# Attention's operands prepared once behind their projection, and a projection moved beside the first attention

## The chip, the cores and the metric

One core of a Trainium2 chip runs the whole kernel. The metric is the device time of one execution in microseconds (us). The kernel before takes 3615.32 us (median of three runs, 3614.81 to 3616.18).

## What is computed

One decoder layer on a prompt of 2048 tokens and on 8 further single tokens (the sample) with a paged cache. Shortened from the reference:

```python
h = rms_norm(x, norm1_g)
aq, ak, av, iq, ik, iw, rq, rf, ri, rg = split(h @ w_in)      # 1024 -> all widths
aq, ak = rms_norm(aq by heads of 64), rms_norm(ak)            # 8 query, 2 key heads
att = attend(aq, ak, av, iq, ik, iw)    # 256 best causal keys by the indexer's score,
                                        # softmax(q.k / 8) over them, times values
rec, S = hgrn2_mixer(rq, rf, ri, rg)    # gated linear recurrence, 4 heads of 128
x = x + concatenate([att, rec]) @ w_out
x = x + square(relu(rms_norm(x) @ w_up)) @ w_down
```

The kernel computes in float32. Where TensorE multiplies, each operand is split in two parts (high: rounded to the engine's fp32r type; low: the rest), and products of parts are summed: three matmuls per product in the projections (function mm3), two in attention, where a stationary operand of 128 rows holds high and low parts of 64 values under each other.

## The kernel before, in words

The prompt is 16 tiles (blocks) of 128 tokens; tile 16 is the sample. The stages, in order of time:

1. Attention's projection (project_tile in attn_proj): for each of three column sets ("k": keys, values, indexer keys; "i": indexer queries; "q": queries) a tile's product goes to PSUM, is normalized, and is stored to DRAM: kD, vD, aqD and others.
2. The recurrence (recur) with the indexer's scores beside it, and the early part of the choice of keys.
3. recurrence_out: for the first EARLY = 10 tiles the recurrent half of the output projection, added to x and stored in yD (line 898). Per tile 4 transposes (line 886) and 24 matmuls of 512 columns (lines 127 to 129). Its weights are loaded as four raw pieces (line 876), rounded by ACT and subtracted by POOL (line 878).
4. Three rounds of attention and MLP, over tiles 0 to 5, 6 to 11 and 12 to 16. For tiles at or past EARLY the MLP stage itself does the recurrent half (ks = 8 in place of 4, line 1660). Steps of the sample's attention (picks; its scores are line 1198) run beside them as tracks, stepped by credit.

Attention keeps keys and values of all blocks so far in SBUF (KS, VS). Each round makes them anew: prep_keys loads a key block, ACT writes its high part (line 103, tile kts), POOL the low part (line 104), TensorE makes four transposes (line 89, tile dt), ACT copies the result out (line 920); values are split by ACT and POOL too (lines 921, 922). prep does it for a block's queries (lines 95, 96, tiles aqs and dt; 8 transposes). So 6, 12 and 16 key blocks are made in the three rounds, 34 in all.

The order on each engine is set at build time by a scheduler with priorities: what stands under high_priority goes ahead, and store() issues its DMA on SP at a low priority. attend(...) in round 0 runs under NEAR, far ahead of the rest. DMAs issued by SP and by POOL stand in those engines' instruction streams, so one that waits holds back what stands behind it.

Of the kernel before, what the change touches and what calls it, by code (L numbers as in the profile page):

```python
# [45 lines left out]
def hymba_kernel(ctx, tc, x_prompt, x_sample, cache_k, cache_v, cache_kidx, state_hgrn, page_table,  # L46
# [99 lines left out]
    def trunk(ctx):  # L146
# [20 lines left out]
        with tc.tile_pool(name="pb", bufs=1, reuse_waits="tile") as pb, ExitStack() as qb_:  # L167
            pj_ = ExitStack()
            pj = pj_.enter_context(tc.tile_pool(name="pj", bufs=1, reuse_waits="tile"))
            with tc.high_priority(offset=HIGH):  # L170
                recur = recurrence(pb, pj)
                finish()
            po_.close()
            qb = qb_.enter_context(tc.tile_pool(name="qb", bufs=1, space=PSUM, reuse_waits="tile"))
            qj = pj_.enter_context(tc.tile_pool(name="qj", bufs=1, space=PSUM, reuse_waits="tile"))
            with tc.high_priority(offset=MIDDLE):
                recur(qb, qj, pj_.close)
                if EARLY:
                    with tc.tile_pool(name="pf", bufs=1, reuse_waits="tile") as pf, \
                         tc.tile_pool(name="qf", bufs=1, space=PSUM, reuse_waits="tile") as qf:  # L180
# [6 lines left out]
        pi_.close()  # L187
        pw = ctx.enter_context(tc.tile_pool(name="pw", bufs=1, reuse_waits="tile"))
        loads = mlp_loads(pw, E_IO, E_WB)
# [29 lines left out]

        with tc.high_priority(offset=FIRST):  # L220
            early = Track(choose_all(choose_block, range(AHEAD)), 0)
            early.finish()
# [65 lines left out]
    PREP = 0  # L288
    EARLY = 10
    yD = dram.tile([NB, P, D], F32, name="yD")  # L290
# [8 lines left out]
    def attn_proj(pc, p1, pr):  # L299
# [82 lines left out]
        def project_tile(t, po, q1, IK, hh, hl, i):  # L382
            n = rows(t)
            rs = slice(row0(t), row0(t) + n)
            for kind, (wh, wl, cols) in (("kiq"[i], weights[i]),):
# [3 lines left out]
                def post():  # L389
                    o = po.tile([P, 512], F32, tag="zo", name="zo", bufs=2)  # L390
                    if kind == "k":
                        head_norm(po, ps[:n, 0:128], n, 2, kg, o[:n, 0:128])
                        head_norm(po, ps[:n, 256:320], n, 1, ig, o[:n, 256:320])
                        nc.scalar.copy(o[:n, 128:256], ps[:n, 128:256])
                        nc.vector.tensor_scalar(o[:n, 320:328], ps[:n, 320:328], IW_SCALE, None, op0=OP.mult)
                        store(kD[rs], o[:n, 0:128])
                        store(vD[rs], o[:n, 128:256])
                        store(iwD[rs], o[:n, 320:328])
                        if t < NB:
                            store(nk_prompt[0, 0, rs].rearrange("s k d -> s (k d)"), o[:n, 0:128])  # L400
                            store(nv_prompt[0, 0, rs].rearrange("s k d -> s (k d)"), o[:n, 128:256])
                            store(ni_prompt[0, 0, rs], o[:n, 256:320])
                            sp = split_twice(po, o[:, 256:320], 1, "iks", 2, nc.gpsimd)
                            pk = q1.tile([P, 512], F32, tag="ikt", name="ikt", bufs=1)
                            for i in range(2):
                                transpose_part(pk[:, i * P:(i + 1) * P], sp[:, 0, i].rearrange("p a d -> p (a d)"))
                            nc.scalar.copy(IK[:, :, rs], pk[:, :2 * P].bitcast(F32R).rearrange("p (i t) -> p i t", i=2))
                        else:
# [461 lines left out]
    def recurrence_out(pf, qf):  # L870
# [3 lines left out]
        for k in range(4):  # L874
            raw = pf.tile([P, D], F32, tag="raw", name="raw", bufs=2)
            nc.sync.dma_start(raw, w_out[0, 512 + k * P:512 + (k + 1) * P])
            nc.scalar.copy(wh[:, k], raw)
            nc.gpsimd.tensor_tensor(wl[:, k], raw, wh[:, k].bitcast(F32), op=OP.subtract)
        for t in range(EARLY):
# [12 lines left out]
            for hf in range(2):  # L892
                s = slice(hf * 512, (hf + 1) * 512)
                po = qf.tile([P, 512], F32, tag="po", name="po", bufs=2)
                for k in range(4):
# [5 lines left out]
    def attend_all(pk, blocks):  # L901

        LEN = (blocks[-1] + 1) * P
        KS = pk.tile([P, NKV, 2, LEN], F32R, name="KS")
        VS = pk.tile([P, blocks[-1] + 1, NKV, P], F32R, name="VS")
        keys = [0]
        VF = pk.tile([P, WHOLE, NKV, HD], F32, name="VF")

        def prep_keys(p2, q2, b, PT):
            rs = slice(b * P, (b + 1) * P)  # L910
            kt = p2.tile([P, NKV * HD], F32, tag="kt", name="kt", bufs=2)
            nc.sync.dma_start(kt, kD[rs])
            vt = VF[:, b] if b < WHOLE else p2.tile([P, NKV, HD], F32, tag="vt", name="vt", bufs=2)
            nc.sync.dma_start(vt.rearrange("p k d -> p (k d)"), vD[rs])
            sp = split_twice(p2, kt, NKV, "kts", 1, nc.gpsimd)
            ps = q2.tile([P, 512], F32, tag="pt", name="dt", bufs=PT)
            for kv in range(NKV):
                for i in range(2):
                    transpose_part(ps[:, (2 * kv + i) * P:(2 * kv + i + 1) * P], sp[:, kv, i].rearrange("p a d -> p (a d)"))
            nc.scalar.copy(KS[:, :, :, rs], ps.bitcast(F32R).rearrange("p (k i t) -> p k i t", k=NKV, i=2))  # L920
            nc.scalar.copy(VS[:, b, :, 0:HD], vt)
            nc.gpsimd.tensor_tensor(VS[:, b, :, HD:], vt, VS[:, b, :, 0:HD].bitcast(F32), op=OP.subtract)

        def prep(p2, q2, cols, b, PT):

            rs = slice(b * P, (b + 1) * P)
            while keys[0] <= b:
                prep_keys(p2, q2, keys[0], PT)
                keys[0] += 1
            aq = p2.tile([P, NH * HD], F32, tag="aq", name="aq", bufs=2)  # L930
            nc.sync.dma_start(aq, aqD[rs])
            n = (b + 1) * P
# [7 lines left out]
            sp = split_heads(p2, aq, NH, "aqs", 1, nc.gpsimd)  # L940
            aqT = p2.tile([P, NH, P], F32R, tag="aqT", name="aqT", bufs=2)
            for q in range(0, NH, 4):
                ps = q2.tile([P, 512], F32, tag="pt", name="dt", bufs=PT)
                for j in range(4):
                    transpose_part(ps[:, j * P:(j + 1) * P], sp[:, q + j].rearrange("p a d -> p (a d)"))
                (nc.vector.tensor_copy if q else nc.scalar.copy)(aqT[:, q:q + 4, :],
                                                                 ps.bitcast(F32R).rearrange("p (h t) -> p h t", t=P))
            return aqT, MB

        def logits(p2, q2, cols, b, u, aqT, MB, LB, out):  # L950
# [4 lines left out]
            for j in range(2):  # L955
                L = p2.tile([P, cols], F32, tag="L", name="L", bufs=LB)
                mx = None
                for k0 in range(0, n, 512):
                    kn = min(512, n - k0)
                    ps = q2.tile([P, 512], F32, tag="lg", name="lg", bufs=2)  # L960
                    for i in range(2):
                        nc.tensor.matmul(ps[:, :kn], aqT[:, 2 * u + j], KS[:, u // 2, i, k0:k0 + kn], start=i == 0, stop=i == 1)  # L962
                    m2 = p2.tile([P, 1], F32, tag="mx", name="mx", bufs=8)
# [10 lines left out]
        def values(p2, q2, b, u, att, PTB, OB, sm, *Ls):  # L974
# [3 lines left out]
            for k0 in range(0, b + 1, 2):  # L978
# [15 lines left out]
                for i in range(m):  # L994
# [4 lines left out]
                    else:  # L999
                        nc.tensor.matmul(O, VS[:, kb, kv], ph[:, s], start=kb == 0, stop=False)  # L1000
                        nc.tensor.matmul(O, VS[:, kb, kv], pl[:, s], start=False, stop=kb == b)
                yield
# [758 lines left out]
```

## Time and profile before

| profiled execution | 3615.09 us (span 3613.4) |
|---|---|
| mean granted TensorE clock | 0.963 of full speed |
| busy, share of the span | PE 93%, PEld 81%, DVE 65%, ACT 62%, POOL 33% |
| projection | 0 to 320 us |
| recurrence, indexer scores | 320 to 1072 |
| recurrence_out, 10 tiles | 1055 to 1126 |
| attention and MLP, round 0 | 1126 to 1286, to 1986 |
| attention and MLP, round 1 | 1986 to 2232, to 2903 |
| attention and MLP, round 2 | 2903 to 3140, to 3613 |

PE is the matmul stream of TensorE, PEld its weight loads, which overlap. A high busy share alone does not say that PE sets the time of a stage: matmuls in a row are pipelined, and a lone one counts with its whole latency. Where PE waits, the row that ends the wait names who was late.

### The profile page before, as it was taken

Reading aid. Unit: us, or ns where it says so; the run is one execution under the profiler, and the core shown is the slowest. Engines: PE = TensorE matmul, PEld = TensorE weight load, DVE = VectorE, ACT = ScalarE, POOL = GpSimd, SP = SyncE. Lnnn points to the kernel's source line nnn. Section 1 sums busy time; section 2 is a strip of 40 time slices with the busy share of each in tenths; the row PEclk is TensorE's granted clock in tenths of the full one; section 3 lists DMA queues with packets and bytes.
Section 4 is the critical chain, followed back from the end, with each engine's and each line's share of the span. In section 5 each row is a group of like instructions: output and inputs, shape, how many; then the busy total and the mean of one; then the engine's idle time right before and its main releaser. Section 6 shows DMA issues by size and latency. Waiting matters only on the chain. (4 is left out here: it accounts for less than half of the span.)

```text
span 3613.4 us, 57448 instructions
## 1 busy us (share of the span) xinstructions
PE 3346.2 (93%) x20446; PEld 2930.4 (81%) x20446; DVE 2333.3 (65%) x5138; ACT 2236.6 (62%) x4121; POOL 1206.7 (33%) x1469
## 2 busy tenths in 40 slices
PE   8998989999998979999999798899799969899999
PEld 7876888899986568888888576888689958788888
DVE  3667788877763656897964578888537448633223
ACT  5788976776753757859832677476695347533332
POOL 5555666554452234444522211113401120011110
PEclk9999999999997989999999899999899979999999
DMA  6546465545445135545544202433434420144554
GB/s 203 147 145 155 140 178 154 154 126 159 129 131 164 57 135 179 167 150 175 163 139 152 65 24 85 135 111 110 154 108 145 135 94 25 62 152 164 186 165 145
DMA packets 345230, 484.90 MB, mean 134 GB/s; under 512 B 39432, under 2 KB 255216, under 8 KB 344816
## 3 DMA queue, kind: packets, MB, share of 16 engines
q1 hardware_dynamic: 287616, 329.37, 28.8%
q0 software_dynamic: 57328, 151.87, 14.2%
q8 instruction: 160, 2.62, 0.3%
q14 instruction: 126, 1.03, 0.1%
HBM read 366.86 MB, written 114.29 MB: 133 GB/s over the span
## 5 line engine op out<-in xcount | busy, mean ns | idle before, releaser
L480 ACT ACTIVATE jkA<-S,candA 128x1152 int8<-128x1152 f32 (+11 forms) x448 | 584.8, 1306 | 116.2 <-DVE candA L484 96.0
L1717 DVE TENSOR_TENSOR y<-y,dn 128x512 f32<-128x512 f32 x512 | 346.1, 683 | 331.1 <-PE dn L129 327.8
L127 PE MATMUL up<-hh,wh 128*128 128x384 f32 (+2 forms) x1536 | 493.4, 321 | 15.0 <-ACT rl L1690 6.9
L128 PE MATMUL up<-hl,wh 128*128 128x384 f32 (+2 forms) x1536 | 491.3, 320 | 0.0
L129 PE MATMUL up<-hh,wl 128*128 128x384 f32 (+2 forms) x1536 | 486.2, 320 | 2.5 <-DMA wl<-low 1.7
L128 PE MATMUL dn<-dl,uh 128*128 128x512 f32 x1024 | 406.5, 397 | 7.2 <-DMA dl<-low 7.2
L127 PE MATMUL dn<-dh,uh 128*128 128x512 f32 x1024 | 403.1, 398 | 10.1 <-DVE y L1717 9.6
L129 PE MATMUL dn<-dh,ul 128*128 128x512 f32 x1024 | 401.2, 394 | 0.0
L127 PEld LDWEIGHTS up<-hh,wh 128*128 128x128 f32 x1536 | 291.9, 190 | 26.7 <-ACT rl L1690 7.4
L128 PEld LDWEIGHTS up<-hl,wh 128*128 128x128 f32 x1536 | 292.2, 190 | 9.0 <-issue 0.3
L129 PEld LDWEIGHTS up<-hh,wl 128*128 128x128 f32 x1536 | 290.1, 190 | 10.5 <-DMA wl<-low 2.0
L1538 ACT CAST dh<-raw 128x1024 fp32r<-128x1024 f32 x96 | 96.9, 1046 | 242.9 <-PE dn L129 231.1
L1693 DVE TENSOR_TENSOR ul<-rl,uh 128x384 fp32r<-128x384 f32 (+1 forms) x192 | 120.7, 629 | 191.7 <-ACT uh L1692 190.5
L127 PEld LDWEIGHTS dn<-dh,uh 128*128 128x128 f32 x1024 | 193.4, 189 | 48.8 <-DVE y L1717 12.3
L129 PEld LDWEIGHTS dn<-dh,ul 128*128 128x128 f32 x1024 | 193.7, 189 | 43.7
L128 PEld LDWEIGHTS dn<-dl,uh 128*128 128x128 f32 x1024 | 194.1, 190 | 40.6 <-DMA dl<-low 7.7
L458 DVE SCALAR_TENSOR_TENSOR sl<-ix,iw,sl 128x512 f32<-128x512 f32 (+3 forms) x266 | 180.5, 678 | 68.0 <-ACT ix L454 65.1
L1690 ACT ACTIVATE rl<-up 128x384 f32<-128x384 f32 (+1 forms) x192 | 86.8, 452 | 214.5 <-PE up L129 204.3
L452 PE MATMUL ix<-IK,iqT 128*128 128x512 f32 (+3 forms) x608 | 189.1, 396 | 27.6 <-DVE sl L458 19.1
L962 PE MATMUL lg<-KS,aqT 128*128 128x512 f32 (+3 forms) x640 | 202.0, 412 | 12.4 <-DVE mx L964 9.6
L454 ACT ACTIVATE ix<-ix,iw 128x512 f32<-128x512 f32 (+3 forms) x304 | 180.5, 597 | 32.4 <-PE ix L452 31.6
L1237 POOL DMA_INDIRECT kg<-in_cache_kidx_dram,pti x128 | 130.0, 1015 | 187.0 <-DVE kt L1239 161.8
(496 smaller groups left out, 9380.4 us busy)
## 6 DMA issues: line engine op xcount, KB each, us to landing
raw<-in_w_up_dram SPq DMA_DIRECT2D x96, 512.0 KB
raw<-in_w_down_dram SPq DMA_DIRECT2D x96, 512.0 KB
wl<-low POOLq DMA_DIRECT2D x76, 512.0 KB
raw<-in_w_in_dram SPq DMA_DIRECT2D x256, 128.0 KB
dl<-low POOLq DMA_DIRECT2D x64, 512.0 KB
wl<-lowp POOLq DMA_DIRECT2D x48, 512.0 KB
low<-wl SPq DMA_DIRECT2D x40, 512.0 KB
low<-dl SPq DMA_DIRECT2D x32, 512.0 KB
```

Of the source, the lines that this page charges most:

```text
L127: nc.tensor.matmul(ps, lh, rh, start=first, stop=False)
L128: nc.tensor.matmul(ps, lh, rl, start=False, stop=False)
L129: nc.tensor.matmul(ps, ll, rh, start=False, stop=last)
L452: nc.tensor.matmul(ps[:, :kn], iqT[:, h], IK[:, i, k0:k0 + kn], start=i == 0, stop=i == 1)
L454: nc.scalar.activation(r[:, :kn], ps[:, :kn], AF.Relu, scale=iw[:, 1, h:h + 1])
L458: nc.vector.scalar_tensor_tensor(sl, r[:, :kn], iw[:, 2, h:h + 1], sl, op0=OP.mult, op1=OP.add)
L480: nc.scalar.activation(jk[:, :n], S[:, :n], AF.Sign, bias=cand.bitcast(F32), scale=-1.0, accum_out=cnt)
L962: nc.tensor.matmul(ps[:, :kn], aqT[:, 2 * u + j], KS[:, u // 2, i, k0:k0 + kn], start=i == 0, stop=i == 1)
L1237: nc.gpsimd.indirect_dma_start(out=kg_, out_offset=None, in_=kview, in_offset=bass.IndirectOffsetOnAxis(ap=pti[:, b, g, u:u + 1], axis=0))
L1538: nc.scalar.copy(wh, raw)
L1693: nc.vector.tensor_tensor(ul[:, o], rl[:, :cn], uh[:, o].bitcast(F32), op=OP.subtract)
L1717: front["dve"] = nc.vector.tensor_tensor(ys_[t][:, s], ys_[t][:, s], po, op=OP.add)
```

## The change

Behind the projection each prompt tile's keys, values and queries are split at once, keys and queries are transposed (4 and 8 transposes a tile, in PSUM tag ikt, now two banks), and all are stored in attention's layout in DRAM: ksD, vsD, qsD. Attention loads them by DMAs that POOL issues, keys and values in chunks of 4 blocks (1 MB and 0.5 MB), queries 0.5 MB a block. recurrence_out now covers all 16 tiles and stands beside round 0's attention, at the default priority, with one raw and one PSUM buffer in place of two. The sample's first track is no longer stepped along that attention, only along the MLP behind it. Cut to its core:

```diff
+    ksD = dram.tile([NB // 4, P, NKV, 2, 512], F32, name="ksD")      # vsD, qsD likewise
@@ trunk
                 recur(qb, qj, pj_.close)
-                if EARLY:
-                    with tc.tile_pool(name="pf", ...) as pf, tc.tile_pool(name="qf", ...) as qf:
-                        recurrence_out(pf, qf)
...
-        along(high(attend(GROUPS[0], 5, 2, 2), NEAR), first)
+        with tc.tile_pool(name="pf", ...) as pf, tc.tile_pool(name="qf", ...) as qf:
+            along(high(attend(GROUPS[0], 4, 2, 2), NEAR))
+            recurrence_out(pf, qf)
         along(mlp(GROUPS[0]), choice, first)
-    EARLY = 10
+    EARLY = 16
@@ project_tile, kind "k", prompt tiles
+    sp = split_twice(po, o[:, 0:128], NKV, "kts", 1, nc.gpsimd)
+    pk = q1.tile([P, 512], F32, tag="ikt", name="ikt", bufs=2)
+    # 4 x transpose_part(pk[...], sp[...])
+    kt = po.tile([P, 512], F32, tag="kt", name="kt", bufs=1)
+    nc.scalar.copy(kt, pk)
+    store(ksD[t // 4, :, :, :, t % 4 * P:(t % 4 + 1) * P], kt...)
+    nc.scalar.copy(vt[:, :, 0], ov)
+    nc.gpsimd.tensor_tensor(vt[:, :, 1], ov, vt[:, :, 0].bitcast(F32), op=OP.subtract)
+    store(vsD[t // 4, :, t % 4], vt...)
@@ kind "q"
-    store(aqD[rs], o[:n])
+    if t == NB:
+        store(aqD[rs], o[:n]); return
+    sp = split_heads(po, o, NH, "aqs", 1, nc.gpsimd)
+    for q in range(0, NH, 4):
+        pq = q1.tile([P, 512], F32, tag="ikt", name="aqt", bufs=2)
+        # 4 x transpose_part(pq[...], sp[...])
+        (nc.vector.tensor_copy if q else nc.scalar.copy)(qt, pq)
+        store(qsD[t, :, q:q + 4], qt...)
@@ recurrence_out: raw bufs 2 -> 1, po bufs 2 -> 1
@@ attend_all: prep_keys and the query split are gone
+    nc.gpsimd.dma_start(aqT, qsD[b])
+    while keys[0] <= b // 4:
+        c = keys[0]
+        nc.gpsimd.dma_start(KS[c], ksD[c, :, :, :, :w])
+        nc.gpsimd.dma_start(VS[c], vsD[c, :, :w // P])
```

How the order of instructions moves is shown at three places. First, TensorE's stream where the first attention begins. Before, recurrence_out's last matmuls (po, th, tl) stand ahead of the key and query transposes (dt) and the first logits (lg):

```order
L129 MATMUL po<-wh,tl 128x512
L89 MATMUL dt<-identr,kts 128x128 x4
L89 MATMUL dt<-identr,aqs 128x128 x8
L89 MATMUL dt<-identr,kts 128x128 x4
L962 MATMUL lg<-KS,aqT 128x128 x4
L89 MATMUL dt<-identr,aqs 128x128 x8
L962 MATMUL lg<-KS,aqT 128x128 x4
L985 MATMUL pt<-ident,L 128x128 x2
L962 MATMUL lg<-KS,aqT 128x128 x6
L998 MATMUL O<-ph,VF 64x256
```

After, with names of its lines (974 is lg, 997 pt, 1010 O, 915 and 127 recurrence_out):

```order
L832 MATMUL po<-Sc,qe 128x128
L974 MATMUL lg<-KS_13767,aqT 128x128 x8
L997 MATMUL pt<-ident,L 128x128
L974 MATMUL lg<-KS_13767,aqT 128x128 x2
L997 MATMUL pt<-ident,L 128x128
L974 MATMUL lg<-KS_13767,aqT 128x128 x4
L1010 MATMUL O<-ph,VF 64x256
L974 MATMUL lg<-KS_13767,aqT 128x128 x2
L915 MATMUL tp<-ident,rt 128x128 x4
L1020 MATMUL ob<-ident,ot 128x64 x2
L997 MATMUL pt<-ident,L 128x128 x2
L127 MATMUL po<-wh,th 128x512
```

The first logits stand directly behind the last matmul of the recurrence (line 832), and recurrence_out's matmuls stand between attention's.

Second, SP's stream at the recurrence's end. Before, the loads of recurrence_out's weights (raw):

```order
L135 DMA recD<-rec 128x4x128
L876 DMA raw<-in_w_out_dram 128x1024 x2
L881 DMA rt<-recD 128x512
L883 DMA y<-in_x_prompt_dram 128x1024
L881 DMA rt<-recD 128x512
L883 DMA y<-in_x_prompt_dram 128x1024
L462 DMA scoreD<-sl 128x512
L881 DMA rt<-recD 128x512
L876 DMA raw<-in_w_out_dram 128x1024
L881 DMA rt<-recD 128x512
```

After; the first raw load stands nine rows above these, right behind the last recD store:

```order
L910 DMA rt<-recD 128x512
L905 DMA raw<-in_w_out_dram 128x1024
L910 DMA rt<-recD 128x512
L135 DMA low_15776<-wl 128x1024
L1062 DMA attD<-att 128x512
L1577 DMA mix<-attD 128x512
L905 DMA raw<-in_w_out_dram 128x1024
L955 DMA MB<-mbD 128x512
L905 DMA raw<-in_w_out_dram 128x1024
```

The third and fourth raw loads stand behind the store of attention's first block (attD) and a load that reads it back (mix).

Third, POOL's stream where the second attention begins. Before, behind the last weight load of the MLP (wl):

```order
L1540 DMA wl<-low_15600 128x1024
L104 TENSOR_TENSOR kts<-kt,kts 128x2x128
L922 TENSOR_TENSOR VS<-VF,VS 128x2x64 x2
L104 TENSOR_TENSOR kts<-kt,kts 128x2x128
L922 TENSOR_TENSOR VS<-VF,VS 128x2x64 x3
L922 TENSOR_TENSOR VS<-vt,VS 128x2x64
L104 TENSOR_TENSOR kts<-kt,kts 128x2x128
L922 TENSOR_TENSOR VS<-vt,VS 128x2x64
L96 TENSOR_TENSOR aqs<-aq,aqs 128x8x64
```

After:

```order
L1552 DMA wl<-low_16052 128x1024
L1552 DMA wl<-low_16185 128x1024
L942 DMA aqT<-qsD 128x1024
L946 DMA KS_23015<-ksD 128x2048
L947 DMA VS_23018<-vsD 128x1024
L946 DMA KS_23016<-ksD 128x2048
L947 DMA VS_23019<-vsD 128x1024
L942 DMA aqT<-qsD 128x1024
L946 DMA KS_23017<-ksD 128x2048
L947 DMA VS_23020<-vsD 128x1024
```

In place of POOL's subtractions stand the DMA issues for queries, keys and values.

## Rows read from the trace of the kernel before

**Rows 1.** Windows: us, then each engine's busy (instructions), PEclk, DMA share, GB/s

```profile
100.00:300.00 200.00, 193.52 (x995) 161.50 (x994) 137.50 (x423) 164.57 (x411) 103.84 (x142) 1.00 0.50 146
...
1072.50:1126.50 54.00, 53.27 (x245) 43.29 (x244) 19.10 (x33) 5.82 (x10) 4.53 (x7) 1.00 0.64 214
...
1126.50:1168.00 41.50, 28.75 (x111) 18.93 (x112) 14.53 (x79) 21.46 (x68) 20.08 (x27) 0.55 0.42 125
...
1168.00:1286.00 118.00, 103.75 (x539) 68.07 (x540) 72.19 (x226) 82.86 (x193) 28.70 (x42) 0.99 0.20 58
...
1986.50:2010.00 23.50, 7.45 (x36) 5.05 (x35) 0.69 (x1) 9.62 (x27) 11.99 (x21) 0.58 0.53 160
...
2010.00:2232.00 222.00, 205.84 (x1292) 164.43 (x1290) 168.22 (x477) 156.65 (x297) 33.28 (x62) 0.98 0.08 24
...
2903.50:2943.00 39.50, 13.50 (x61) 8.79 (x60) 0.69 (x1) 14.86 (x38) 16.08 (x27) 0.57 0.42 127
...
3140.00:3230.00 90.00, 78.50 (x619) 76.08 (x620) 27.90 (x52) 30.50 (x52) 10.27 (x23) 0.91 0.51 166
```

**Rows 2.** PE timeline into first attention: start, us, line, op; idle before in brackets

```profile
1126.04 0.39 PE L129 MATMUL po<-wh,tl 128*128 128x512 f32 x1
...
1137.81 1.25 PE L89 MATMUL dt<-identr,aqs 128*128 128x128 f32 x8 [5.71 <-POOL aqs L96]
...
1139.79 0.43 PE L962 MATMUL lg<-KS,aqT 128*128 128x128 f32 x1
```

**Rows 3.** PE timeline into second attention

```profile
1986.28 0.39 PE L129 MATMUL dn<-dh,ul 128*128 128x512 f32 x1
...
2010.22 1.21 PE L962 MATMUL lg<-KS,aqT 128*128 128x512 f32 x2
```

**Rows 4.** PE timeline into third attention

```profile
2903.34 0.39 PE L129 MATMUL dn<-dh,ul 128*128 128x512 f32 x1
...
2911.91 0.37 PE L89 MATMUL dt<-identr,kts 128*128 128x128 f32 x1 [8.18 <-ACT kts L103]
...
2943.15 1.21 PE L962 MATMUL lg<-KS,aqT 128*128 128x512 f32 x2
```

**Rows 5.** PE timeline, two tiles of the recurrence's output projection

```profile
1090.04 0.60 PE L886 MATMUL tp<-ident,rt 128*128 128x128 f32 x4
...
1095.97 0.60 PE L886 MATMUL tp<-ident,rt 128*128 128x128 f32 x4
```

**Rows 6.** PE timeline, one key block's transposes

```profile
1180.70 0.53 PE L89 MATMUL dt<-identr,kts 128*128 128x128 f32 x4
```

**Rows 7.** Windows of line 1198 alone (the sample's scores): PE, PEld, clock, DMA

```profile
1126.50:1286.00 159.50, 12.24 (x40) 7.18 (x40) 0.87 0.25 76
```

**Rows 8.** Operations by tile (aqs, kts, KS): count, ns min/median/max, first and last start

```profile
L95 ACT CAST aqs<-aq x16: 610/622/643, 1135.8 to 2998.9; 128x512 fp32r<-128x512 f32 x16
...
L96 POOL TENSOR_TENSOR aqs<-aq,aqs x16: 1261/1276/1297, 1136.5 to 2999.6; 128x512 fp32r<-128x512 f32 x16
...
L103 ACT CAST kts<-kt x34: 404/407/425, 1130.2 to 2998.1; 128x256 fp32r<-128x256 f32 x34
...
L920 ACT CAST KS<-dt x34: 578/586/597, 1132.5 to 3047.4; 128x512 fp32r<-128x512 f32 x34
```

**Rows 9.** Page, part 3: packets, MB, share of 16 engines

```profile
q0 software_dynamic: 57328, 151.87, 14.2%
```

**Rows 10.** SP timeline: query stores of two projection tiles, recurrence's last store

```profile
205.62 0.33 SPq L135 DMA_DIRECT2D aqD<-zo  x1
...
225.55 0.33 SPq L135 DMA_DIRECT2D aqD<-zo  x1
...
1077.42 0.37 SPq L135 DMA_DIRECT2D recD<-rec  x1
```

**Rows 11.** POOL timeline: two weight splits; one DMA issue

```profile
1065.86 4.69 POOL L878 TENSOR_TENSOR wl<-raw,wh 128x1024 fp32r<-128x1024 f32 x2
...
1986.58 0.58 POOL L1540 DMA_DIRECT2D wl<-low  x1 [12.95 <-issue]
```

More of the change, by code (lines that the diff above doesn't have):

```diff
@@ L139, in hymba_kernel @@
     mbD = dram.tile([NB, P, SEQ], BF, name="mbD")
+    ksD = dram.tile([NB // 4, P, NKV, 2, 512], F32, name="ksD")
+    vsD = dram.tile([NB // 4, P, 4, NKV, P], F32, name="vsD")
+    qsD = dram.tile([NB, P, NH, P], F32, name="qsD")
     NG = 4
@@ L187, in trunk @@
         pi_.close()
+        with tc.high_priority(offset=FIRST):
+            early = Track(choose_all(choose_block, range(AHEAD)), 0)
+            early.finish()
         pw = ctx.enter_context(tc.tile_pool(name="pw", bufs=1, reuse_waits="tile"))
@@ L218, in along @@
                         t.step()
-        with tc.high_priority(offset=FIRST):
-            early = Track(choose_all(choose_block, range(AHEAD)), 0)
-            early.finish()
         choice = Track(choose_all(choose_block, range(AHEAD, GROUPS[2][0])), PACE[0])
         first = Track(part(), PUMP[0])
-        along(high(attend(GROUPS[0], 5, 2, 2), NEAR), first)
+        with tc.tile_pool(name="pf", bufs=1, reuse_waits="tile") as pf, \
+             tc.tile_pool(name="qf", bufs=1, space=PSUM, reuse_waits="tile") as qf:
+            along(high(attend(GROUPS[0], 4, 2, 2), NEAR))
+            recurrence_out(pf, qf)
         along(mlp(GROUPS[0]), choice, first)
@@ L414, in post @@
                         head_norm(po, ps[:n], n, NH, qg, o[:n])
-                        store(aqD[rs], o[:n])
+                        if t == NB:
+                            store(aqD[rs], o[:n])
+                            return
+                        sp = split_heads(po, o, NH, "aqs", 1, nc.gpsimd)
+                        for q in range(0, NH, 4):
+                            pq = q1.tile([P, 512], F32, tag="ikt", name="aqt", bufs=2)
+                            for j in range(4):
+                                transpose_part(pq[:, j * P:(j + 1) * P], sp[:, q + j].rearrange("p a d -> p (a d)"))
+                            qt = po.tile([P, 512], F32, tag="qt", name="qt", bufs=2)
+                            (nc.vector.tensor_copy if q else nc.scalar.copy)(qt, pq)
+                            store(qsD[t, :, q:q + 4], qt.rearrange("p (h t) -> p h t", t=P))
                     else:
@@ L874, in recurrence_out @@
         for k in range(4):
-            raw = pf.tile([P, D], F32, tag="raw", name="raw", bufs=2)
+            raw = pf.tile([P, D], F32, tag="raw", name="raw", bufs=1)
             nc.sync.dma_start(raw, w_out[0, 512 + k * P:512 + (k + 1) * P])
@@ L893, in recurrence_out @@
                 s = slice(hf * 512, (hf + 1) * 512)
-                po = qf.tile([P, 512], F32, tag="po", name="po", bufs=2)
+                po = qf.tile([P, 512], F32, tag="po", name="po", bufs=1)
                 for k in range(4):
@@ L903, in attend_all @@
         LEN = (blocks[-1] + 1) * P
-        KS = pk.tile([P, NKV, 2, LEN], F32R, name="KS")
-        VS = pk.tile([P, blocks[-1] + 1, NKV, P], F32R, name="VS")
+        NC = (blocks[-1] + 4) // 4
+        KS = [pk.tile([P, NKV, 2, min(512, LEN - 512 * c)], F32R, name=f"KS{c}") for c in range(NC)]
+        VS = [pk.tile([P, min(4, LEN // P - 4 * c), NKV, P], F32R, name=f"VS{c}") for c in range(NC)]
         keys = [0]
[L907 to L922, printed above, removed]
@@ L924, in prep @@
-        def prep(p2, q2, cols, b, PT):
-            rs = slice(b * P, (b + 1) * P)
-            while keys[0] <= b:
-                prep_keys(p2, q2, keys[0], PT)
+        VF = pk.tile([P, WHOLE, NKV, HD], F32, name="VF") if blocks[0] < WHOLE else None
+        def prep(p2, q2, cols, b, PT):
+            aqT = p2.tile([P, NH, P], F32R, tag="aqT", name="aqT", bufs=2)
+            nc.gpsimd.dma_start(aqT, qsD[b])
+            while keys[0] <= b // 4:
+                c = keys[0]
+                w = KS[c].shape[3]
+                nc.gpsimd.dma_start(KS[c], ksD[c, :, :, :, :w])
+                nc.gpsimd.dma_start(VS[c], vsD[c, :, :w // P])
+                if c == 0 and VF is not None:
+                    nc.sync.dma_start(VF.rearrange("p b k d -> p b (k d)"),
+                                      vD[0:WHOLE * P].rearrange("(b p) d -> p b d", p=P))
@@ L939, in prep @@
                                         fill=NEG, base=0, channel_multiplier=1)
[L940 to L947, printed above, removed]
             return aqT, MB
@@ L961, in logits @@
                     for i in range(2):
-                        nc.tensor.matmul(ps[:, :kn], aqT[:, 2 * u + j], KS[:, u // 2, i, k0:k0 + kn], start=i == 0, stop=i == 1)
+                        nc.tensor.matmul(ps[:, :kn], aqT[:, 2 * u + j], KS[k0 // 512][:, u // 2, i, :kn], start=i == 0, stop=i == 1)
                     m2 = p2.tile([P, 1], F32, tag="mx", name="mx", bufs=8)
@@ L999, in values @@
                     else:
-                        nc.tensor.matmul(O, VS[:, kb, kv], ph[:, s], start=kb == 0, stop=False)
-                        nc.tensor.matmul(O, VS[:, kb, kv], pl[:, s], start=False, stop=kb == b)
+                        nc.tensor.matmul(O, VS[kb // 4][:, kb % 4, kv], ph[:, s], start=kb == 0, stop=False)
+                        nc.tensor.matmul(O, VS[kb // 4][:, kb % 4, kv], pl[:, s], start=False, stop=kb == b)
                 yield
```

19 lines of the change are left out of this document (12 added, 7 removed).

## Prediction

> **What bounds the kernel now.** I read the windows by stage first, then TensorE's (PE's) timeline where each stage begins, then the durations of the operations that the change moves. In the windows [rows 1] the reader is to see two kinds of stretch. In the long ones PE is nearly full at the full granted clock: 193.52 of 200 us in the projection, 53.27 of 54 in recurrence_out, 205.84 of 222 in the second attention. There work taken from PE comes off the time, and work added to it goes on. At the start of each attention PE is busy 28.75 of 41.5, 7.45 of 23.5 and 13.5 of 39.5 us, and the granted clock is 0.55 to 0.58, near the lower of its two levels (1.2 of 2.4 GHz). These starts are where attention prepares its operands: from the last matmul of the stage before to the first logits pass 13.8 us [rows 2], 23.9 us [rows 3] and 39.8 us [rows 4]. The brackets in rows 2 and 4 name POOL and ACT splits as what PE waits for. In the third start 13 key blocks go by between 2911.91 and 2943.15, 2.40 us a block, though a block's four transposes take 0.53 us [rows 6]: the loop ACT rounds, POOL subtracts, PE turns, ACT copies sets the pace. So the change works on PE work in full stages, and on three starts that no PE work fills.
>
> **The change part by part.** I sum against the profiled execution, 3615.09 us (span 3613.4 and 1.7 around it); the median of the runs, 3615.32, is the same for this purpose.
>
> 1. *Projection.* Added per prompt tile: 12 transposes, 192 in all, at 0.53/4 = 0.13 us [rows 6]: 25 us on a PE that idles only 6.5 of 200 us [rows 1]. ACT gets per tile the key cast 0.41, the key copy-out 0.59, the query cast 0.62 [rows 8], one query copy like the key copy 0.59, and a value cast of about 0.3 (half the elements of the key cast's output and some fixed part): 2.5 us. A tile takes 225.55 - 205.62 = 19.9 us [rows 10] and ACT is busy 82% of it, so it has 3.6 us free: it fits, without much to spare. POOL (52% busy) gets 1.28 and 0.72 [rows 8] and a value subtraction, the second query copy falls to DVE (69%), and SP gets stores of 0.9 MB a tile in place of 0.4 MB, on a DMA share of 0.50. I take +25. Bounds: +17 if a third fills PE's gaps, +51 if ACT cannot go above its 82% (16 x 2.6 = 42 us, over 0.82).
>
> 2. *From the recurrence's end to the first MLP's start* (1072.5 to 1286: 213.5 us). Removed: recurrence_out by itself, 54 us, the start gap of 13.8, the sample's scores, 12.24 us of PE [rows 7], and 72 transposes (6 key blocks x 4, 6 query blocks x 8), 9.5 us. Added beside attention: 16 tiles of recurrence_out at 1095.97 - 1090.04 = 5.93 us [rows 5], 95 us. If nothing of it found a gap: attention without its start and the samples, 159.5 - 13.3 - 12.2 = 134, plus 95 is 229 us. If PE were full throughout: 95 and some 85 us of attention's own matmuls is 180 (28.75 us at a clock of 0.55 and 103.75 at 0.99 [rows 1] are 118 at the full one; less 12.2 and 9.5; less some 12, my estimate, for lone matmuls counted with their latency, 0.39 [rows 2] against (5.93 - 0.53)/24 = 0.225 in a row). Against the lower end: recurrence_out's weights come late. Before, the split of two pieces ran on POOL at 1065.86, during the recurrence [rows 11]; now the first raw load stands behind the last recD store (1077.42 before [rows 10]), the pieces share one buffer, so each of four waits for load, ACT's cast and POOL's 2.35 us, and pieces three and four stand on SP behind the store of attention's first block and the load that waits for it. Queued behind them are the later blocks' masks (MB). I put the filler's start at 35 to 40 us behind the recurrence's end; until then attention's first block runs alone, with the clock low. Then 95 us of filler and some 75 us of attention nearly pack PE: 37 + 95 + 75 = 207. I take 207, so -6.5, with 180 to 229.
>
> 3. *First MLP.* The sample's steps that ran beside the first attention now run here, where PE is otherwise full: +12 (their scores [rows 7]), 0 if PE's waits in the MLP take them, 20 with their smaller steps.
>
> 4. *Second attention.* The start waits for loads only: 0.5 MB of queries and two chunks of keys and values, 3.5 MB. The software queue moved 151.87 MB in 14.2% of 16 engines' 3613.4 us [rows 9], so 296 GB/s with all engines on it: 12 us. By the order's waits the first chunk goes behind three stores of 0.5 MB and DVE, so its buffer lies where the MLP's y stood: 5 us at the same rate. 17 us for all, 10 for queries and chunk 0, with which the first logits can run: I take 14 of 23.9, so -10, with -18 (the stores done early) and 0. Behind the start 40 query and 20 key transposes go, 60 x 0.13 = -8, on a PE that is 93% busy.
>
> 5. *Third attention.* Four chunks and the queries are 6.5 MB, 22 us at 296 GB/s. The first logits need 1.5 MB of it, but the first head's pass cannot end before the last chunk: about 23 of 39.8 us stay as loss, -17, with -32 (the loads all ahead of the MLP's end) and 0. Steady: 24 query and 12 key transposes, -5.
>
> 6. *Second and third MLP.* Their tiles 10, 11 and 12 to 15 lose the recurrent half, 5.93 us each: -12 and -24. I take -10 and -18, because at the third MLP's start PE is idle or at a lower clock for a tenth of 90 us [rows 1] and waits there for loads that stay.
>
> Sum: 25 - 6.5 + 12 - 10 - 8 - 17 - 5 - 10 - 18 = -37.5, so 3577.6; I say 3578.
>
> **Where a page speaks against it.** A DMA that POOL issued took POOL 0.58 us in the trace [rows 11], with DVE at work in the MLP. The Trainium skill (SBUF — State Buffer, section "SBUF: two separate sides") says that a DMA issued from GpSimd has its descriptors written through a port that VectorE's two-port operations lock, and that the SP or ACT queue is free of this: by it, moving these loads from SP to POOL costs. The row shows no such stall, so the sum keeps the rate of rows 9. The same notes (DMA: Bandwidth & Descriptors, section "Anatomy of one DMA — SWDGE (gpsimd) path") put such a DMA at about 2 us and its bytes at 436 GB/s; an estimate by that page makes the 6.5 MB of step 5 some 17 us, and the sum about 5 us lower; the measured 296 GB/s decides.
>
> **The rivals.**
> - *The projection becomes ACT's.* For: 82% before, the order of its queue is fixed, and 2.5 us a tile come on. Against: 3.6 us a tile were free. Then step 1 is +51, the sum 3578 + 26 = 3604.
> - *The preparation loop stalls the projection (the slower side).* The loop that paces the third start now runs in the projection, through two PSUM banks and ACT's in-order queue: 2.4 us a key block [rows 4], and for a query block 0.62 + 1.28 [rows 8], 1.06 of transposes and a copy 0.59, 3.6 us. If PE's in-order stream waits for all of it, a tile costs 6.0 us, 16 tiles 96 in place of 25: 3578 + 71 = 3649. It turns the result where the stall is over 37.5/16 = 2.3 us a tile above step 1. For: PE has no slack, and a transpose behind a late split holds the next tile's products. Against: the scheduler can put a tile's products between split and transpose, with three banks for them.
> - *The filler isn't hidden:* step 2 at 229, 3578 + 22 = 3600. For: ACT (82.86 of 118 us) and DVE serve both chains, po has one bank. Against: PE is idle there now.
> - *The loads don't beat the preparation:* POOL's queue or the stores hold the chunks, steps 4 and 5 lose 27 at the starts: 3605. Against: 1.5 MB a chunk at 296 GB/s is 5 us.
> - *All overlaps work:* step 1 at +17, step 2 at 190, chunk 0 alone awaited: -8, -17, -8: 3545.
>
> **How the numbers follow.** Forecast 0.43, all overlaps 0.11, ACT's projection 0.14, loop 0.13, unhidden filler 0.13, loads 0.06. This kernel's measurement tells about 0.2% from no change, 7 us, so faster ends at 3608. The forecast's own range is 3555 to 3598, all faster. ACT's projection, the filler and the loads lie near 3600 to 3605 and give 0.23 faster, 0.08 same, 0.02 slower; all overlaps is faster; the loop gives 0.02 same, 0.11 slower. Faster 0.43 + 0.11 + 0.23 = 0.77, same 0.10, slower 0.13. A range from 3530 to 3612 leaves out the loop and little else.
>
> **What would show it.** Step 1: the projection's tile pitch at 21.5 us (rival: 23, ACT above 90%; or 24 and more with PE waiting for POOL's aqs or kts). Step 2: first logits within some us of the recurrence's end, and recurrence_out's products between attention's; 207 us to the MLP's start. Steps 4 and 5: behind the last dn PE loses some 14 and 23 us, to DMAs of KS and VS and not to ACT or POOL. Step 6: both later MLPs shorter by 10 and 18. A slower kernel with the projection unchanged in pitch would make the argument wrong as a whole.

## The result, and the profile after

The changed kernel takes 3577.01 us (median of four runs, 3575.78 to 3582.42) against 3615.75 for the kernel before in the same runs: ratio 0.9891, 95% interval 0.9874 to 0.9909. Predicted were 3578. The profiled execution is the longest of the four, 3582.42 us with a span of 3580.7; against the span before it is 32.7 us shorter, where the forecast summed to 37.5.

The windows of the changed kernel by stage (length, then busy us and instructions of PE, PEld, DVE, ACT, POOL; granted clock; DMA share; GB/s):

```profile
100.00:300.00 200.00, 192.69 (x1059) 162.64 (x1057) 135.01 (x397) 174.21 (x439) 119.46 (x167) 1.00 0.56 165
1081.50:1140.00 58.50, 48.71 (x211) 31.09 (x211) 18.61 (x95) 31.42 (x90) 18.67 (x20) 0.85 0.51 174
1140.00:1260.00 120.00, 120.00 (x596) 88.70 (x595) 48.70 (x142) 45.88 (x102) 4.58 (x11) 1.00 0.41 138
1999.00:2012.00 13.00, 0.48 (x3) 0.25 (x2) 0.69 (x1) 0.00 (x0) 5.19 (x10) 0.63 0.97 333
2012.00:2222.00 210.00, 196.74 (x1216) 157.45 (x1217) 165.53 (x472) 140.88 (x268) 22.09 (x50) 0.97 0.14 45
2902.50:2912.30 9.80, 0.44 (x3) 0.07 (x1) 0.69 (x1) 0.00 (x0) 5.12 (x10) 0.72 0.98 329
2912.30:2945.00 32.70, 21.95 (x109) 16.12 (x110) 17.88 (x56) 12.06 (x18) 1.39 (x3) 0.72 0.50 192
3121.00:3182.00 61.00, 44.69 (x324) 40.88 (x323) 24.28 (x45) 20.20 (x34) 16.31 (x22) 0.87 0.57 183
```

Against [rows 1]: in the projection ACT rose from 164.57 to 174.21 of 200 us and PE stays full, so the loops of the preparation hold nothing up for long. Beside the first attention PE is busy all of 120 us, where it had 28.75 of 41.5 and 103.75 of 118. At the starts of the later attentions ACT and DVE now do next to nothing, POOL's 5.19 and 5.12 us are the issues of ten loads each, and the DMA share is 0.97 and 0.98: a start that three engines paced has become one that the transfer paces.

The PE timeline of the changed kernel at the three starts, which answers to [rows 2 to 4] (start, us, line, operation; in brackets the idle time before it and what ended it):

```profile
1081.21 0.39 PE L832 MATMUL po<-Sc,qe 128*128 128x128 f32 x2
1081.35 0.64 PE L974 MATMUL lg<-KS,aqT 128*128 128x128 f32 x4
...
1090.49 1.11 PE L915 MATMUL tp<-ident,rt 128*128 128x128 f32 x4 [0.19 <-DMA rt<-recD]
...
1092.28 0.80 PE L127 MATMUL po<-wh,th 128*128 128x512 f32 x1
```

```profile
1998.87 0.39 PE L129 MATMUL dn<-dh,ul 128*128 128x512 f32 x1
2011.78 1.19 PE L974 MATMUL lg<-KS,aqT 128*128 128x512 f32 x2 [12.52 <-DMA KS<-ksD]
```

```profile
2912.26 1.19 PE L974 MATMUL lg<-KS,aqT 128*128 128x512 f32 x2 [9.36 <-DMA KS<-ksD]
2918.25 1.19 PE L974 MATMUL lg<-KS,aqT 128*128 128x512 f32 x2 [4.80 <-DMA KS<-ksD]
2921.97 1.19 PE L974 MATMUL lg<-KS,aqT 128*128 128x512 f32 x2 [2.52 <-DMA KS<-ksD]
2925.64 1.62 PE L974 MATMUL lg<-KS,aqT 128*128 128x128 f32 x4 [2.48 <-DMA KS<-ksD]
```

The first logits follow the recurrence at once, and recurrence_out begins 9 us behind them. From the last matmul of the MLP to the first logits it is 12.9 us in place of 23.9, and 9.7 in place of 39.8 (the last dn stands at 2902.5), with three further waits of 4.80, 2.52 and 2.48 us for key chunks, 19.2 us of waits in all at this start. All of them end with a DMA of KS.

To see where time went and came from I cut each trace at the same matmuls of PE: the last of the projection (psp), the recurrence's last (po of line 832), the first transposes (tp of mix) and last product (dn) of each MLP. Stages in us, of one profiled execution each:

| kernel | projection | recurrence | to MLP 1 | MLP 1 | attention 2 | MLP 2 | attention 3 | MLP 3 |
|---|---|---|---|---|---|---|---|---|
| before | 326.4 | 745.8 | 213.7 | 700.3 | 242.8 | 674.3 | 234.6 | 470.4 |
| changed | 344.9 | 736.4 | 208.9 | 708.7 | 223.6 | 680.1 | 218.5 | 454.7 |
| changed, again (e0) | 344.5 | 739.6 | 210.5 | 708.1 | 224.8 | 681.9 | 218.3 | 450.9 |
| preparation alone (e1) | 346.0 | 737.7 | 202.7 | 703.6 | 224.1 | 680.9 | 217.4 | 468.8 |
| 16 tiles at recurrence's end (e2) | 344.6 | 734.6 | 239.5 | 702.5 | 225.8 | 683.9 | 217.0 | 451.3 |
| 10 tiles beside attention (e3) | 346.7 | 731.5 | 182.2 | 709.7 | 223.8 | 682.0 | 216.2 | 471.1 |
| sample paced faster (e4) | 347.1 | 732.5 | 210.3 | 708.2 | 224.0 | 672.1 | 218.6 | 450.7 |
| keys before values (e5) | 343.6 | 730.6 | 208.8 | 706.8 | 224.7 | 685.0 | 211.5 | 450.6 |
| loads on SP (e6) | 344.0 | 729.3 | 208.5 | 708.8 | 226.8 | 681.1 | 217.6 | 451.3 |
| 12 tiles, sample paced faster (e7) | 344.4 | 731.2 | 193.9 | 708.4 | 225.3 | 672.8 | 215.2 | 468.8 |
| low parts on SP (e8) | 342.5 | 729.3 | 208.7 | 706.9 | 222.2 | 652.2 | 215.3 | 451.3 |
| low parts on SP, keys first (e9) | 346.0 | 737.6 | 208.5 | 707.1 | 222.5 | 648.8 | 213.2 | 450.0 |
| 10 tiles, low parts on SP (e10) | 348.0 | 738.2 | 179.0 | 710.1 | 222.7 | 674.8 | 219.8 | 465.0 |
| before, low parts on SP (e11) | 326.2 | 746.8 | 218.4 | 700.7 | 241.9 | 672.5 | 235.3 | 469.4 |

Here MLP 1 to 3 are the MLPs of rounds 0 to 2. One line of it goes against the forecast: the second MLP lost the recurrent half of two tiles and yet grew, from 674.3 to 680.1. In e1, where it keeps the work of before, it is 680.9.

### The profile page after: what moved, and what is told of

It reads as the page before. It is cut to its first block, busy times and chain, and to the rows that moved or that the text cites. A ratio compares the mean times of both kernels' runs of the same rounds, so it can differ in the third digit from the quotient of the medians.

```text
span 3580.7 us, 56788 instructions
## 1 busy us (share of the span) xinstructions
PE 3321.7 (93%) x20230; PEld 2911.3 (81%) x20230; DVE 2341.7 (65%) x5150; ACT 2212.5 (62%) x4063; POOL 1198.9 (33%) x1463
## 5 line engine op out<-in xcount | busy, mean ns | idle before, releaser
L1729 DVE TENSOR_TENSOR y<-y,dn 128x512 f32<-128x512 f32 x512 | 346.7, 682 | 304.6 <-PE dn L129 302.5
L1705 DVE TENSOR_TENSOR ul<-rl,uh 128x384 fp32r<-128x384 f32 (+1 forms) x192 | 117.2, 611 | 199.0 <-ACT uh L1704 197.7
L983 ACT ACTIVATE L<-L,nm 128x128 f32<-128x128 f32 (+15 forms) x128 | 154.2, 1205 | 119.6 <-DVE nm L982 118.7
L483 ACT ACTIVATE ix<-ix,iw 128x512 f32<-128x512 f32 (+3 forms) x304 | 182.2, 603 | 50.8 <-PE ix L481 50.2
L1702 ACT ACTIVATE rl<-up 128x384 f32<-128x384 f32 (+1 forms) x192 | 86.8, 452 | 194.8 <-PE up L129 192.3
```

The source lines that it names most:

```text
L483: nc.scalar.activation(r[:, :kn], ps[:, :kn], AF.Relu, scale=iw[:, 1, h:h + 1])
L983: nc.scalar.activation(L[:, :n], L[:, :n], AF.Exp, bias=nm, scale=ATT_SCALE, accum_out=sm[:, j:j + 1])
L1705: nc.vector.tensor_tensor(ul[:, o], rl[:, :cn], uh[:, o].bitcast(F32), op=OP.subtract)
L1729: front["dve"] = nc.vector.tensor_tensor(ys_[t][:, s], ys_[t][:, s], po, op=OP.add)
```

## The experiments

Runs e0 to e3, e4 to e7, e8 with e9, and e10 with e11 shared a chip each and the runs of the kernel before, so their ratios can be compared; medians across them less so (the medians of the kernel before were 3618.7 to 3628.8 us on them).

**Which part gives what: e0 to e3.** e0 is the changed kernel unchanged. e1 has only the preparation (the hunks of project_tile and attend_all); in e1 and e2 the sample's first track also stays beside the first attention, as before. e2 and e3:

```diff
e2: e1, with
-    EARLY = 10
+    EARLY = 16
e3: the changed kernel, with
-    EARLY = 16
+    EARLY = 10
```

> The changed kernel once more, as the base for the runs beside it. 3574 to 3582 us, ratio 0.989. If the gather theory holds (one 28 us wait of TensorE at 2551 us of the changed trace for a weight load that POOL issues behind 32 gathers), its length should vary between executions, since 20 us of it hang on when the sample's indices arrive; if it is a fixed cost it is within 2 us of the first trace.

> Only the preparation moves behind the projection; recurrence_out stays at the recurrence's end with 10 tiles, and the sample's steps stay beside the first attention. Theory A (the preparation is the gain): projection +18, first attention -18 (start and transposes), second -19, third -16: about 3580. Theory B (the gain is recurrence_out beside the first attention, the preparation pays for itself at best): 3600 or more.

> As the run with the preparation alone, but recurrence_out does all 16 tiles at the recurrence's end. Theory A: the products only move between full stages, 6 x 5.93 = 36 us more there, 12 and 16 to 24 us less in the second and third MLP: 0 to +8 against the preparation alone. Theory B: against the changed kernel it is slower by what the overlap brings, 15 us or more.

> The changed kernel with EARLY = 10: recurrence_out beside the first attention, for 10 tiles. If the stretch beside attention is packed (TensorE busy 40 of 40 us in the changed trace from 1140 to 1260) six tiles less shorten it by 36 us and the later MLPs get 28 to 36 back: -8 to 0 against the changed kernel. If the six tiles were hidden in attention's gaps, the stretch shortens by under 15 us and the kernel is slower by 15 us or more.

Measured: e0 3579.30, ratio 0.9878 [0.9856, 0.9900]; e1 3588.84, 0.9905 [0.9880, 0.9929]; e2 3605.57, 0.9961 [0.9945, 0.9977]; e3 3564.49, 0.9839 [0.9819, 0.9859].

Theory A held: the preparation alone brings 0.95 of the 1.22% (the two intervals overlap). By the table it costs 19.6 us at the projection's end, of which the recurrence gives back 8.1, and it saves 11.0, 18.7 and 17.2 us in the three attentions; 3.3 and 6.6 go on in the first two MLPs. e2 lost 17 us against e1, where I had allowed 8: it adds 36.8 us at the recurrence's end, gets 17.5 back in the third MLP and nothing in the second. e3 is 15 us faster than e0, beyond the 8 that I allowed: 28.3 us come off the stretch beside attention, as a packed stretch should give, 20.2 go on in the third MLP, and again nothing in the second. That is 8; another 6 lie in projection and recurrence, where these kernels do the same and single executions differ by as much. Putting the products beside attention, and the sample's first track behind it, is worth 0.83% with 16 tiles (e2 to e0) and 0.66% with 10 (e1 to e3). The windows show it: from the recurrence's end to the first MLP in e2, recurrence_out and then attention by itself,

```profile
1079.20:1176.00 96.80, 91.35 (x413) 74.71 (x412) 31.71 (x50) 9.57 (x16) 5.27 (x6) 0.96 0.66 223
1176.00:1318.70 142.70, 123.15 (x581) 79.27 (x580) 82.64 (x299) 90.61 (x231) 39.34 (x62) 0.88 0.31 94
```

and in the changed kernel, both in one stretch:

```profile
1081.30:1290.20 208.90, 196.30 (x964) 142.89 (x963) 81.27 (x272) 91.01 (x218) 25.82 (x37) 0.96 0.41 141
```

PE's 196.30 busy us of 208.90 leave little more to fill. So why do 16 tiles, which move 36 us of work out of the later MLPs, lose against 10? The second MLP's first part, up to its first up product, did shorten with 16 tiles, from 94.1 us in e3 to 72.7 in the changed kernel; the rest of it grew by as much.

**The second MLP: e4 and e8.** The trace of the changed kernel shows one long wait in it. POOL, and PE's row behind it:

```profile
2529.68 1.10 POOL L1473 DMA_INDIRECT KG<-in_cache_k_dram,idx  x1 [20.05 <-DVE idx L1462]
...
2574.54 0.94 POOL L1473 DMA_INDIRECT VG<-in_cache_v_dram,idx  x1 [0.30 <-issue]
2575.48 1.21 POOL L1552 DMA_DIRECT2D dl<-low  x2
```

```profile
2579.74 0.80 PE L128 MATMUL dn<-dl,uh 128*128 128x512 f32 x1 [28.27 <-DMA dl<-low]
```

POOL stands still 20.05 us in front of the first of 32 gathers of the sample's chosen keys (KG) and values (VG), because their indices (idx) are not there, needs 46 us to issue them, and only then issues the loads of the MLP's low parts (dl, wl) that stand behind them in its stream. PE waits 28.27 us for one of them. Around it PE is busy 6.78 of 40 us, with the granted clock at 0.57:

```profile
2545.00:2585.00 40.00, 6.78 (x23) 4.98 (x22) 18.67 (x48) 22.44 (x24) 26.34 (x26) 0.57 0.53 175
```

Before, the same gathers began with an idle time of 0.87 us, and PE's wait behind them was 7.22:

```profile
2525.67 1.62 POOL L1461 DMA_INDIRECT KG<-in_cache_k_dram,idx  x1 [0.87 <-DVE idx L1450]
```

```profile
2580.39 0.80 PE L128 MATMUL dn<-dl,uh 128*128 128x512 f32 x1 [7.22 <-DMA dl<-low]
```

In e0 the wait was 31.92 us and POOL's idle time 19.87, so the wait varied, but not by the arrival of the indices, to which I had put it.

The order on POOL says why. Before, and in e1 and e3, four weight loads stand between the sample's last table work (ol) and the gathers; with 16 tiles the last ol stands directly in front of KG:

```
e3:  ol<-o,keyb / dl<-low / dl<-low / wl<-low / wl<-low / KG x16 / VG x16 / dl<-low
changed:  dl<-low / wl<-low / wl<-low / ol<-o,keyb / KG x16 / VG x16 / dl<-low
```

The indices are no later than they were: from the end of the last ol to the first gather it is 19.6 us before and 20.1 in the changed kernel. Before, POOL spent 14 of these waiting to issue the first of the four loads, whose buffer PE still read:

```profile
2520.04 0.59 POOL L1540 DMA_DIRECT2D dl<-low  x1 [13.97 <-PE dn L129]
```

So the change is in what POOL issues within that time. From one dl load to the next, across the gathers, it is 52.5 us before and 69.8 in the changed kernel.

e4 paces the sample so that the order is as in e3; e8 takes the loads off POOL's stream in the second MLP alone:

```diff
e4:
-    PACE, PUMP = (12000, 14000), (8000, 9000)
+    PACE, PUMP = (12000, 14000), (8000, 8400)
e8, in mlp_loads, for the second MLP:
-                nc.gpsimd.dma_start(wl, lowD[key])
+                nc.sync.dma_start(wl.bitcast(F32), lowD[key])
```

> The changed kernel with one number different: the sample's second track is stepped every 8400 columns of the MLP instead of 9000, which puts its last table work ahead of four weight loads on POOL, as it stood before the change, and the 32 gathers behind them. Gather theory: POOL no longer stands idle 20 us in front of the gathers, TensorE's wait for the weight load behind them falls from 28 to 32 us to 7 to 13 us, the second MLP shortens by 15 to 20 us, and the whole to about 3560. Rival (the second MLP is longer with 16 tiles for another reason): the wait moves or stays and the time stays within 5 us of 3578.

> The changed kernel with the second MLP's loads of the weights' low parts issued by SP in place of POOL, so that none stands behind the sample's gathers. Gather theory: TensorE's wait of 28 to 32 us for the low part goes and the second MLP, 680 to 682 us in the changed kernel, falls to about 655 to 660; the whole to about 3555. Rival (the low parts are late for lack of DMA bandwidth beside the gathers, or SP's queue holds them as long): the wait stays above 15 us and the second MLP above 670.

Measured: e4 3572.81, ratio 0.9855 [0.9827, 0.9882]; e8 3539.02, 0.9781 [0.9763, 0.9799]. What POOL and PE wait for in e4, and PE in e8 (us in all, times, longest):

```profile
POOL KG L1473 <- DVE idx L1462: 6.1, 1, 6.1
```

```profile
PE dn L128 <- DMA dl<-low: 23.8, 1, 23.8
```

```profile
PE up L129 <- DMA wl<-low: 3.7, 3, 2.0
```

e4 did half of what it was to do: POOL's idle time fell from 20 to 6.1 us, PE's wait only to 23.8, the second MLP by 8 to 10 us. From one dl load to the next, across the gathers, it is 60.5 us there: the 46 us of gathers themselves are enough to make a load late. The time of the whole does not decide it, because e4's four runs spread from 3562.51 to 3581.56 us and its interval overlaps that of e0. In e8 no dl is waited for at all, the second MLP takes 652.2 us, 28 less than in the changed kernel, and the whole is about 1% faster than e0, 35 to 40 us. In the table 28 to 30 of these are the second MLP's; most of the rest lies in projection and recurrence, which the edit leaves alone. The rival (bandwidth beside the gathers) is out: the gathers are still there, and POOL still idles 22.93 us in front of them. It is the place in POOL's stream: in the changed kernel dl was issued at 2575.48 and PE went on at 2579.74, 4.3 us later.

**Is it SP's queue as such, and do 16 tiles pay then: e10 and e11.** The edit of e8, on e3 and on the kernel before.

> EARLY = 10 beside the first attention with the second MLP's low parts loaded by SP. With the wait behind the gathers gone on both sides, only the place of six tiles' products differs from the run with 16 tiles: first attention's stretch 28 us shorter, the start of the second MLP 18 to 21 us longer (its two tiles and the other half of the output weights), the third MLP 18 longer: about 3547, 8 us slower than with 16 tiles. If ten tiles stay faster, as they were with the loads on POOL (3564 against 3579), the gathers were not why 16 tiles lost: 3530 or less.

> The kernel before with only the second MLP's low parts loaded by SP. Its trace shows one wait of 7.2 us behind the gathers: 8 to 12 us faster, about 3605. If the gain of 39 us on the changed kernel comes from SP's queue as such and not from the gathers, 25 us or more here too.

Measured: e10 3563.29, ratio 0.9823 [0.9807, 0.9839]; e11 3616.67, 0.9969 [0.9959, 0.9980]. On the kernel before the edit gives 0.3%, about 11 us, the size expected and far from the 25 of SP's queue as such. Its wait of 7 us is gone, but the second MLP is only 1.8 us shorter in the profiled execution (672.5), so where the 11 us lie is not shown. With 10 tiles the edit gives about 6 us against e3; with 16 tiles 35 to 40. With the wait gone 16 tiles are faster than 10 by 0.42% (e10 to e8), 15 us, where they were 0.39% slower with it (e3 to e0). I had expected 8. The two profiled executions differ by more, 29 us: by the table 29.7 us go on beside attention, 22.6 and 13.7 come off the later MLPs and 4.5 off the third attention, 11 in all; 14 lie in projection and recurrence, which the edit leaves alone and whose sum varies from 1072 to 1086 us in the table. So the sign is shown, and a size beyond some 10 us is not.

**The starts: e5, e6, and e7, e9 for the sum.** The edits, e9 being e8 with that of e5 and e7 being e4 with EARLY = 12:

```diff
e5:
-                nc.gpsimd.dma_start(KS[c], ...); nc.gpsimd.dma_start(VS[c], ...)   # chunk by chunk
+            for c in fresh: nc.gpsimd.dma_start(KS[c], ...)
+            for c in fresh: nc.gpsimd.dma_start(VS[c], ...)
e6:
-            nc.gpsimd.dma_start(aqT, qsD[b])                     # KS, VS likewise
+            nc.sync.dma_start(aqT.bitcast(F32), qsD[b])
```

> The changed kernel with all key chunks of an attention's start issued ahead of the value chunks. If the loads are served in order and the starts are bound by bytes (the changed trace moves about 400 GB/s there), the last key chunk comes 0.5 MB earlier in the second and 1.5 MB earlier in the third attention: 1.3 and 3.8 us, -3 to -5 in all. If the queue shares its engines among all chunks: 0. If values become late: TensorE's O waits for VS, 0 to +3.

> The changed kernel with the loads of queries, keys and values issued by SP in place of POOL. Bytes theory: the starts are bound by the transfer, so within 4 us of the changed kernel, unless SP's queue has stores in front of them, which makes it slower. Rival (descriptors written by POOL hold the loads back): waits for KS at the two starts, 15 and 19 us, fall by a third or more and the time by 8 us or more.

> EARLY = 12 beside the first attention, with the sample's track at 8400. If a tile costs the packed stretch its full 5.93 us and is worth 4 to 5 us in the third MLP, but 10 us each for tiles 10 and 11 in the second MLP (which then also loads only half of the output weights): four tiles less than the run with 8400 and 16 tiles, -24 + 17 = -7 against that; about 3553. If the last four tiles were covered by attention, +10 or more against it.

> The run before with the key chunks issued ahead of the value chunks as well. The two act in different stages, so the effects add: the third attention 211 to 213 us in place of 218, the whole about 3549. If they don't add, as the run before.

Measured: e5 3578.40, ratio 0.9875 [0.9858, 0.9891]; e6 3576.21, 0.9864 [0.9847, 0.9880]; e7 3566.58, 0.9837 [0.9821, 0.9853]; beside e8, e9 3540.74, 0.9780 [0.9764, 0.9796]. PE's wait for keys over all three rounds, in the changed kernel, e5, e6, e8 and e9:

```profile
PE lg L974 <- DMA KS<-ksD: 34.2, 6, 12.5
```

```profile
PE lg L975 <- DMA KS<-ksD: 29.1, 6, 11.9
```

```profile
PE lg L974 <- DMA KS<-ksD: 25.5, 4, 11.1
```

```profile
PE lg L977 <- DMA KS<-ksD: 33.0, 6, 11.1
```

```profile
PE lg L978 <- DMA KS<-ksD: 27.7, 6, 10.8
```

In e5 the wait shrinks by 5 us, in e9 by as much against e8, and the third attention takes 211.5 us in place of 218.5, in e9 213.2 in place of e8's 215.3, but no time of the whole can be told from the kernel without it, in either pair: 0.9875 against 0.9878 (another chip), 0.9780 against 0.9781. For the whole it is inconclusive. e6 lowers the wait for keys to 25.5 us, but moves it rather than removes it: the mask (MB) of the third attention's first block now stands on SP behind the keys, DVE waits for it and PE for DVE.

```profile
2921.87 0.69 DVE L976 CUSTOM_DVE_ANT_0 L<-lg,MB 128x512 f32<-128x512 f32 x1 [22.19 <-DMA MB<-mbD]
```

```profile
2922.62 1.58 PE L974 MATMUL lg<-KS,aqT 128*128 128x512 f32 x4 [9.29 <-DVE mx L976]
```

The first logits of the third start come after 9.9 us (9.7 from POOL), and the time is within the interval of the others. So no sign shows that the loads were held back by being POOL's, though the masks keep e6 from being a clean test of it.

e7 came 13 us higher than expected. It reads 6 below e4, which is within e4's own spread. By the table its four tiles fewer take 16.4 us off beside attention and put 18.1 on in the third MLP, so nothing shows that these four pay either way; what 16 tiles lost against 10 points to the two tiles of the second MLP, whose gain the wait behind the gathers took.

e8 and e9 are the fastest: 2.2% faster than the kernel before, twice the gain of the change.

## Why the prediction was right, and where it was not

The total came out by luck as well as by the mechanism: two terms were wrong by the same amount in opposite directions. Term by term, the forecast and the table:

- *Projection*, forecast +25: +18.5 at its end and +9.0 at the recurrence's end (e1, where recurrence_out stays: +19.6 and +11.5). The mis-sized term is the price of a transpose. I divided one group of four by four, 0.13 us; the changed trace has groups of eight and of four,

```profile
208.96 0.80 PE L89 MATMUL aqt<-identr,aqs 128*128 128x128 f32 x8
...
215.36 0.46 PE L89 MATMUL ikt<-identr,kts 128*128 128x128 f32 x4
```

so four more cost 0.34, 0.085 each, 16 us for 192: a group's time holds some 0.12 us that is paid once. The rest is that the recurrence is 8 us shorter in e1; PE's idle time in it falls by only 2 us (55.7 to 53.6), so why is not shown. Nor did the pitch tell much: I took 19.9 us from one pair of tiles, but from the first to the last query store of the 16 prompt tiles the mean is 18.6 before and 19.4 after, where I had put 21.5. Neither ACT (87% busy) nor the loop of the preparation decided: PE has 192.69 busy us of 200, where it had 193.52.

- *Recurrence's end to the first MLP*, -6.5: -4.8. The stretch was 209 where I said 207. The last weights came as late as I had put it: PE still waits for wh (the second time 41 us behind the recurrence's end):

```profile
1112.02 0.80 PE L127 MATMUL po<-wh,th 128*128 128x512 f32 x1 [2.45 <-ACT wh L906]
...
1121.98 0.50 PE L127 MATMUL po<-wh,th 128*128 128x512 f32 x1 [0.77 <-ACT wh L906]
```

But products with the first pieces begin at 1092 and not with the last, and from 1140 on the stretch is packed, as forecast.

- *First MLP*, +12: +8.4, of which e1, which leaves the sample beside attention, has 3.3.

- *Second attention*, -18: -19.2. *Third attention*, -22: -16.1. Both starts wait for KS and nothing else. In the third, from the issue of the first load (queries, at 2902.86) to the logits behind the last key chunk (2925.64) it is 22.8 us, where I had put 22 for the loads. The rate of 296 GB/s was near what these loads got; in the 22 us from 2904:

```profile
GB/s 149 387 313 365 335 350 298 328 402 417 387 439 395 362 414 411 405 406 450 407 438 390 422 387 394 432 462 402 462 432 380 395 439 469 447 402 432 365 417 410
...
q0 software_dynamic: 1415, 7.28, 88.7%
q1 hardware_dynamic: 432, 1.41, 17.3%
```

POOL's queue moved 7.28 MB, 331 GB/s, and all queues together 8.69 MB, 395 GB/s, since masks (MB) and y stores on SP's queue share the time. The Trainium skill (DMA: Bandwidth & Descriptors, section "Anatomy of one DMA — SWDGE (gpsimd) path") gives bytes over 436 GB/s behind some 2 us; the 17 us that I estimated by that page are further from the 22.8 than my 22. PE's waits at this start are 19.2 us, fewer than the 23 that I had forecast as loss. What I left out stands behind them: from the first logits to the MLP, without the 9.8 us of further waits for keys, it is 199.0 us where it was 194.8, and I had taken 5 off. Part of it is the clock: from 2912.3 to 2945 PE is busy 21.95 us at a granted clock of 0.72, and by an estimate from that row some 6 of them are owed to the clock. The rest is open.

- *Second MLP*, -10: +5.8. This step failed. Its first part shortened by 12.1 us as worked out (84.8 to 72.7), but I priced the stage by the work that leaves it and did not ask what its earlier end does to POOL's stream: PE's wait behind the gathers went from 7.22 to 28.27 us. I had named that rule for the starts (a wait holds what is queued behind it) and not for the gathers, of which the trace before had a first sign, the 7.22 us above. e8 shows that the whole 28 us were there to be had. Two things more were not in the sum. The preparation alone makes the stage 6.6 us longer (e1, with ten tiles and a wait of 10.75 us behind the gathers). And that the 12.1 agree is luck: e1's first part is 93.8 us, 9.0 more than before with the same work, for a reason that no run here shows, and the two tiles then took off 21. *Third MLP*, -18: -15.7.

The sum of the errors: -16 for projection and recurrence, -4 for the first MLP, +6 for the third attention, +16 for the second MLP, +2.8 for the rest: 4.8 us. The other rule that I weighed, descriptors locked out by VectorE (the Trainium skill, SBUF — State Buffer, section "SBUF: two separate sides"), does not show at the starts: POOL issued most of the loads there in 0.54 us each, and on SP (e6) they were not measurably better. But VectorE is busy only 0.69 of 13 us there, so these rows hardly test it, and neither did the one row that I went by. In the second MLP what made POOL the wrong engine for a load was what stood in front of it.

## What to carry to other kernels

Work taken out of a stage moves everything else on each in-order engine against it: look at which waiting or long run of instructions the loads behind it will now meet. Price a short instruction by the difference between two group sizes, not by dividing one group. An overlap is worth its idle time only until the engine is full; beyond that, moved work is moved cost, and its sign hangs on what the other stage does with the room.

## What had not been expected of the hardware

One indirect gather of 128 rows holds POOL for 0.94 to 2.4 us (KG median 0.95 in the changed kernel) and the next begins 0.30 us later, so 32 of them keep every DMA that POOL has to issue back for 46 us; the same loads issued by SP went past them (e8). Around one such wait of 28 us the granted clock was 0.57 over 40 us. The first products behind it were slow too: dn matmuls begin 0.42 to 0.43 us apart until 2582.46, and 0.23 to 0.24 from 2582.77 on.
